# First layer's modulation on TensorE, four products at a time on quarters of its columns; all first shift tiles computed there too

## The chip, the cores and the metric

The kernel runs on one core of a Trainium2 chip. The metric is device time in microseconds, from the start of the program to its end. A core has five engines that work side by side, each through its own queue in order: PE (TensorE, matrix products), DVE (VectorE), ACT (ScalarE), POOL (GpSimd) and SP (SyncE, which here issues the loads). Loads run on 16 DMA engines. Smaller is better.

## The reference

Two transformer blocks of two layers each work on 256 latent tokens and 256 context tokens of width 1024, batch 1. Each layer derives six modulation vectors (shift, scale and gain for the mixer; the same for the feed-forward) from a conditioning vector, once for the latents (c) and once for the context (c_ctx). The first block's mixer is a bidirectional mLSTM beside a gated spatial unit and a convolution; the second block's are attention layers. The part that the change touches is the first layer's first lines:

```
c_act = jax.nn.silu(c)
cc_act = jax.nn.silu(c_ctx)
mod = (c_act @ w_mod[l] + b_mod[l])[:, None, :]
modc = cc_act @ w_mod[l] + b_mod[l]
sh1, sc1, g1, sh2, sc2, g2 = jnp.split(mod, 6, axis=-1)
shc1, scc1, gc1, shc2, scc2, gc2 = jnp.split(modc, 6, axis=-1)
px = (rmsnorm(x, norm1_g[l]) * (1.0 + sc1) + sh1) @ w_in[l] + b_in[l]
pc = (rmsnorm(xc, norm1_g[l]) * (1.0 + scc1) + shc1) @ w_in[l] + b_in[l]
```

All is float32. The projections are computed with both operands split into a high and a low half, three products each.

## The kernel before

The activations lie transposed, channels on partitions: xT is eight tiles [128, 512], the first 256 columns the context tokens, the rest the latents. A modulation vector of 1024 entries is eight tiles of 128 entries (j = 0 to 7 in each of the six parts c of a layer), one entry per partition. There are two ways of computing a tile. `mod_tile` (line 155) loads 128 rows of the transposed weights (512 KB) and takes two dot products on VectorE (line 165, one for each stream) with the conditioning vector spread over all partitions (`cv`). `mod_pe` (line 171) does two tiles for both streams on TensorE: it loads two blocks of 512 KB (line 177), adds up eight products over the channels in float32 (line 180; each product shows as two records), in which the stationary operand has only two columns, the two conditioning vectors; ScalarE copies the resulting two rows (line 182), two transpositions turn them onto the partitions (line 184), and `mod_take` adds the bias and makes the norm's gain (lines 191 and 196).

`start` (line 198) is everything ahead of the first mixer. It loads xT, squares it and sums (lines 212 and 217), spreads the two conditioning vectors over the partitions with products of ones (`cvec_pe`, line 138), and computes scale and shift of the first norm in four steps q of two tiles. All four steps' scales and the shifts of q = 1 (`SHPE`) go over TensorE, five calls of mod_pe; the other six shift tiles are dot products on VectorE. The 512 KB blocks of both kinds share eight buffers. The factors of the norm come from the sums of squares (line 323), a chain of small VectorE operations (from line 294) and a product that spreads them (line 331); xT times the factors is xr (line 242). Then for each of the eight tiles k of channels ScalarE applies scale and shift (line 255), and the result is split into aH (line 378) and aL (line 379). Three weight tiles of the input projection are loaded in the midst of it and split (whi, line 392; wlo, line 397).

The mixer (`mixer1`, line 590) begins with three tiles of the input projection, gates, k0 and k1, whose products (lines 411 to 413, 512 tokens each, named pin) are taken k by k as aH and aL come, 72 in all. The gates then go through a chain of running sums and maxima on VectorE (lines 727 to 755), whose result is transposed on TensorE (line 764). Its constants are loaded from line 597 on into memory that `start` has used, so they wait for its last aL. The rest of the mixer follows the list PLAN. One of its items, `mods`, put behind other work by a priority lowered by 300, calls mod_pe four times for part 4, the scale of the feed-forward's norm; its buffers are the two of `mw`.

The framework orders each engine's instructions ahead of time, by priority (program order, unless changed) and by a cost model's estimate of when operands are ready. Within an engine the order is then fixed. Modulation tiles of later use are queued (`mod_queue`, `work`) and put behind the last split or residual on VectorE (the fence).

## Time and profile before

| | us |
|---|---|
| median of 3 runs | 2062.37 |
| lowest, highest | 2057.48, 2063.44 |
| span of the profiled execution | 2055.1 |

The profiled execution's span runs from its first to its last instruction. The profile gives, for each engine, what it did when, what ended its idle time, and the chain of work that ended last. "x16" counts instructions; a float32 product shows as two records. In rows of the timeline the first number is the start and the second the time to the end of the last one, so neighbouring pipelined products overlap in their durations, and the distance of two starts is what one of them takes of the engine's time. In the rows of stretches each engine has its busy time and its count. The clock column is the granted clock of TensorE as a share of full speed, the last two columns are the load of the DMA engines.

### The profile page before, as it was taken

What the parts mean: (1) busy time and instruction counts of PE and PEld (TensorE: products, weight loads), DVE (VectorE), ACT (ScalarE), POOL (GpSimd) and SP (SyncE); (2) the same over time, 40 slices, a digit from 0 to 9 for tenths busy, and PEclk for the clock granted to TensorE, in tenths of its full rate; (3) what the DMA queues carried; (4) which work ended last, traced back from release to release, by engine and by line L of the source; (5) the groups of instructions that cost most, each with busy time, mean ns of one, the idle gap of its engine ahead of it and who ended that gap; (6) DMA issues with size and microseconds to landing.
All of it is one profiled execution on the core that took longest, in us unless ns stands there. A gap on an engine that the chain in (4) does not pass through costs nothing.

```text
span 2055.1 us, 34137 instructions
## 1 busy us (share of the span) xinstructions
PE 2010.6 (98%) x13196; PEld 1784.5 (87%) x13196; DVE 1545.2 (75%) x3105; ACT 924.5 (45%) x1612; POOL 85.7 (4%) x103
## 2 busy tenths in 40 slices
PE   8999999999999899999999999999999999999999
PEld 3798779888888799999998789888888889999999
DVE  6997789987898768987877667777653487788554
ACT  4324544222322346744556675322222266666443
POOL 0000010000001000200100002000000200001000
PEclk9999999999999999999999999999999999999999
DMA  7532265678766332576651015446752231216554
GB/s 295 181 103 92 97 232 176 211 248 295 235 216 198 111 102 94 170 263 212 202 171 61 22 41 186 154 149 223 260 170 71 70 112 64 73 54 224 182 157 134
DMA packets 98182, 324.22 MB, mean 158 GB/s; under 512 B 11418, under 2 KB 14234, under 8 KB 98020
## 3 DMA queue, kind: packets, MB, share of 16 engines
q1 hardware_dynamic: 98020, 322.04, 47.7%
q8 instruction: 104, 1.70, 0.3%
q14 instruction: 58, 0.48, 0.1%
HBM read 320.95 MB, written 1.05 MB: 157 GB/s over the span
## 4 chain that ended last, share of the span: by engine, by line
PE 89%; DVE 6%; ACT 2%; DMA 1%; issue 1%; SPq 0%; POOL 0%; ACTq 0%; POOLq 0%; DVEq 0%
PE pg L411 6%; PE pd L411 6%; PE pd L413 6%; PE pd L412 6%; PE pu L413 6%; PE pg L412 6%; PE pu L412 6%; PE pg L413 6%; PE pu L411 6%; PE pin L411 5%; PE pin L413 5%; PE pin L412 5%; PE pov L1223 2%; PE ptq L1127 2%; DVE wlo L397 1%; PE po L411 1%
## 5 line engine op out<-in xcount | busy, mean ns | idle before, releaser
L392 ACT CAST whi<-wraw 128x1024 fp32r<-128x1024 f32 (+2 forms) x443 | 429.5, 973 | 797.0 <-PE pu L412 188.9
L397 DVE TENSOR_TENSOR wlo<-wraw,whi 128x1024 fp32r<-128x1024 f32 (+2 forms) x443 | 502.5, 1138 | 155.0 <-ACT whi L392 152.3
L165 DVE CUSTOM_DVE_ANT_0 junk<-mw,cv,modb 128x1024 bf16<-128x1024 f32 x272 | 349.6, 1285 | 51.3 <-DMA mw<-in_modw 45.2
L411 PE MATMUL pd<-hH,whi 128*128 128x256 f32 (+1 forms) x748 | 245.4, 328 | 0.0
L412 PE MATMUL pd<-hL,whi 128*128 128x256 f32 (+1 forms) x748 | 245.1, 328 | 0.0
L413 PE MATMUL pd<-hH,wlo 128*128 128x256 f32 (+1 forms) x748 | 244.8, 327 | 0.0
L411 PE MATMUL pg<-aH,whi 128*128 128x256 f32 (+1 forms) x704 | 233.8, 332 | 0.3 <-ACT aH L374 0.3
L413 PE MATMUL pu<-aH,wlo 128*128 128x256 f32 (+1 forms) x704 | 233.5, 332 | 0.3 <-DVE wlo L397 0.3
L412 PE MATMUL pg<-aL,whi 128*128 128x256 f32 (+1 forms) x704 | 233.6, 332 | 0.0
L412 PE MATMUL pu<-aL,whi 128*128 128x256 f32 (+1 forms) x704 | 233.2, 331 | 0.0
L411 PE MATMUL pu<-aH,whi 128*128 128x256 f32 (+1 forms) x704 | 233.2, 331 | 0.0
L413 PE MATMUL pg<-aH,wlo 128*128 128x256 f32 (+1 forms) x704 | 233.2, 331 | 0.0
L412 PEld LDWEIGHTS pd<-hL,whi 128*128 128x128 f32 x748 | 142.2, 190 | 12.2
L411 PEld LDWEIGHTS pd<-hH,whi 128*128 128x128 f32 x748 | 142.4, 190 | 12.0
L413 PEld LDWEIGHTS pd<-hH,wlo 128*128 128x128 f32 x748 | 142.2, 190 | 12.0
L411 PE MATMUL pin<-whi,aH 128*128 128x256 f32 x512 | 150.0, 293 | 1.4 <-ACT aH L374 1.1
L412 PE MATMUL pin<-wlo,aH 128*128 128x256 f32 x512 | 148.0, 289 | 0.0
L413 PE MATMUL pin<-whi,aL 128*128 128x256 f32 x512 | 147.2, 289 | 0.3 <-DVE aL L375 0.2
L411 PEld LDWEIGHTS pg<-aH,whi 128*128 128x128 f32 x704 | 133.7, 190 | 13.2 <-ACT aH L374 0.5
L413 PEld LDWEIGHTS pu<-aH,wlo 128*128 128x128 f32 x704 | 133.7, 190 | 13.1 <-DVE wlo L397 0.5
L413 PEld LDWEIGHTS pg<-aH,wlo 128*128 128x128 f32 x704 | 133.8, 190 | 12.6
L412 PEld LDWEIGHTS pg<-aL,whi 128*128 128x128 f32 x704 | 133.8, 190 | 12.5
(339 smaller groups left out, 4150.8 us busy)
## 6 DMA issues: line engine op xcount, KB each, us to landing
wraw<-in_wgu SPq DMA_DIRECT2D x176, 512.0 KB, 4.4
mw<-in_modw SPq DMA_DIRECT2D x168, 512.0 KB, 4.2
wraw<-in_win SPq DMA_DIRECT2D x92, 512.0 KB, 3.5
wraw<-in_wdn SPq DMA_DIRECT2D x64, 384.0 KB, 3.5
wraw<-in_wout SPq DMA_DIRECT2D x47, 512.0 KB, 3.5
wraw<-in_wdn SPq DMA_DIRECT2D x64, 320.0 KB, 3.4
mn<-in_modn SPq DMA_DIRECT2D x18, 512.0 KB, 5.6
mn<-in_modw SPq DMA_DIRECT2D x6, 512.0 KB, 7.3
```

Of the source, the lines that this page charges most:

```text
L165: r = nc.vector.tensor_tensor_reduce(out=junk, in0=w, in1=self.cv[s], scale=1.0, scalar=self.mb_t[:, 2 * b + l, j:j + 1], op0=ALU.mult, op ...
L392: nc.scalar.copy(out=hi[:, :n], in_=raw[:, :n])
L397: nc.vector.tensor_tensor(out=lo[:, :n], in0=raw[:, :n], in1=hi[:, :n], op=ALU.subtract)
L411: mm(out=out, lhsT=wh, rhs=xh, start=start, stop=False)
L412: mm(out=out, lhsT=wh, rhs=xl, start=False, stop=False)
L413: mm(out=out, lhsT=wl, rhs=xh, start=False, stop=stop)
L1127: nc.tensor.transpose(out=pt[:, h, :], in_=a.bitcast(F32).rearrange("p e d -> p (e d)"), identity=self.ident)
L1223: nc.tensor.matmul(out=po[64 * b:64 * b + 64, e // 2, :], lhsT=vN[:, kc, 64 * g:64 * g + 64], rhs=u["PT"][:, kc, :], start=kc == 0, stop=k ...
```

## The change

The products of mod_pe go to quarters of TensorE's columns. The stationary operand becomes 32 columns wide, the two conditioning vectors and 30 columns of zeros (`columns`, built once in start and once in mods), and the four products of a block write to four groups of 32 partitions, each of which adds up over the two blocks only. The copy takes all 128 partitions, and instead of a transposition a product with a constant of two columns (`quart`) adds the four quarters and turns the rows. All eight shift tiles of the first norm are computed in this way, so that start makes eight calls of mod_pe and no dot product; their order is no longer tied to the product that spreads the factors. The sums alternate between two banks instead of halves of one. The spreading of the conditioning vectors on TensorE goes; the two spread vectors, which later tiles need, are loaded as broadcasts at the end of start. Three constants are loaded through ScalarE's queue instead of SP's, ahead of the Silu of the small conditioning columns. Comments are dropped as well.

```diff
-CS = {"ident": (0, 128), "mf": (128, 128), "mb": (256, 128)}
-NCS = 384
+CS = {"ident": (0, 128), "mf": (128, 128), "mb": (256, 128), "quart": (384, 2)}
+NCS = 386
...
-SHPE = (1,)
...
-        self.cols = g.tile([128, 4 * KT], F32, name="cols")
+        self.cols = g.tile([128, KT, 2], F32, name="cols")
         nc.sync.dma_start(out=self.cols, in_=i["ccol"])
-        nc.scalar.activation(out=self.cols, in_=self.cols, func=AF.Silu)
         self.cst = g.tile([128, NCS], F32, name="cst")
-        nc.sync.dma_start(out=self.cst, in_=i["cst"])
+        nc.scalar.dma_start(out=self.cst, in_=i["cst"])
         self.ident = self.C("ident")
         self.gn = g.tile([128, 9, KT], F32, name="gn")
-        nc.sync.dma_start(out=self.gn, in_=i["gn"])
+        nc.scalar.dma_start(out=self.gn, in_=i["gn"])
         self.mb_t = g.tile([128, 4, 48], F32, name="modb")
-        nc.sync.dma_start(out=self.mb_t, in_=i["modb"])
+        nc.scalar.dma_start(out=self.mb_t, in_=i["modb"])
+        nc.scalar.activation(out=self.cols, in_=self.cols, func=AF.Silu)
...
-    def cvec_pe(self, s, row):
...
+    def columns(self, pool):
+        t = pool.tile([128, KT, 32], F32, name="cols32")
+        self.nc.gpsimd.memset(t, 0.0)
+        self.nc.vector.tensor_copy(out=t[:, :, 0:2], in_=self.cols)
+        return t
...
-    def mod_pe(self, c, q, room, pr, pm):
+    def mod_pe(self, cols, c, q, room, pr, pm):
         nc = self.nc
         for h in range(2):
             w = room()
             nc.sync.dma_start(out=w, in_=self.i["modn"][PE_C.index(c), q, h])
             for n in range(4):
-                k = 4 * h + n
-                nc.tensor.matmul(out=pr, lhsT=self.cols[:, 2 * k:2 * k + 2], rhs=w[:, 256 * n:256 * n + 256], start=k == 0, stop=k == KT - 1)
-        row = self.np_.tile([128, 256], F32, tag="xn", name="mrow")[0:2, :]
+                nc.tensor.matmul(out=pr[32 * n:32 * n + 32, :], lhsT=cols[:, 4 * h + n, :], rhs=w[:, 256 * n:256 * n + 256],
+                                 start=h == 0, stop=h == 1)
+        row = self.np_.tile([128, 256], F32, tag="xn", name="mrow")
         nc.scalar.copy(out=row, in_=pr)
         for j in (0, 1):
-            nc.tensor.transpose(out=pm[:, 2 * (2 * q + j):2 * (2 * q + j) + 2], in_=row[:, 128 * j:128 * j + 128], identity=self.ident[0:2, 0:2])
+            nc.tensor.matmul(out=pm[:, 2 * (2 * q + j):2 * (2 * q + j) + 2], lhsT=row[:, 128 * j:128 * j + 128], rhs=self.C("quart"),
+                             start=True, stop=True)
...
-            rows = [mf.tile([1, D], F32, name=f"crow{s}") for s in range(2)]
-            for s, row in enumerate(rows):
-                nc.sync.dma_start(out=row, in_=self.i["cvec"][s:s + 1, :])
+            pR = [pR, self.ps.tile([128, T], F32, tag="aux", bufs=1, name="pR1")]
...
-            for s, row in enumerate(rows):
-                self.cvec_pe(s, row)
...
-            def scale(q):
-                for c in (1, 0) if q in SHPE else (1,):
-                    half[0] = 1 - half[0]
-                    self.mod_pe(c, q, room, pR[0:2, 256 * half[0]:256 * half[0] + 256], pM[:, 16 * c:16 * c + 16])
-                    self.mod_take(c, 2 * q, 2 * q + 2, pM[:, 16 * c:16 * c + 16])
-            def shift(j):
-                if j // 2 not in SHPE:
-                    self.mod_tile(0, 0, j, (1, 0), room())
-            for j in range(2):
-                shift(j)
-            scale(0)
+            cols = self.columns(mf)
+            def part(c, q):
+                half[0] = 1 - half[0]
+                self.mod_pe(cols, c, q, room, pR[half[0]][:, 0:256], pM[:, 16 * c:16 * c + 16])
+                self.mod_take(c, 2 * q, 2 * q + 2, pM[:, 16 * c:16 * c + 16])
+            part(1, 0)
+            part(0, 0)
             npb = self.rstd_rows([acc], T, 1.0 / D, pc, pb)
...
             for q in range(4):
-                with self.tc.issue_after(npb.ins):
-                    if q:
-                        scale(q)
-                for j in (2 * q, 2 * q + 1):
-                    if j >= 2:
-                        shift(j)
+                if q:
+                    part(1, q)
+                    part(0, q)
...
+        self.cvecs(0)
...
             def mods():
                 pm = self.mm_tile("pm")
+                cols32 = self.columns(tp)
                 for q in range(4):
-                    self.mod_pe(4, q, lambda: self.mp.tile([128, D], F32, tag="mw", bufs=2, name="mn"), pm[0:2, 0:256], pm[:, 256:272])
+                    self.mod_pe(cols32, 4, q, lambda: self.mp.tile([128, D], F32, tag="mw", bufs=2, name="mn"), pm[:, 0:256], pm[:, 256:272])
                 self.mod_take(4, 0, KT, pm[:, 256:272])
...
+    for n in range(4):
+        for st in range(2):
+            cst[32 * n + st, 384 + st] = 1.0
```

## Rows read from the trace of the kernel before

**Rows 1.** The page: busy us, share, instructions by engine; shares of the last chain.

```profile
PE 2010.6 (98%) x13196; PEld 1784.5 (87%) x13196; DVE 1545.2 (75%) x3105; ACT 924.5 (45%) x1612; POOL 85.7 (4%) x103
...
PE 89%; DVE 6%; ACT 2%; DMA 1%; issue 1%; SPq 0%; POOL 0%; ACTq 0%; POOLq 0%; DVEq 0%
```

**Rows 2.** Busy time by stretch (stretch, its length, engines, granted clock, DMA share, GB/s).

```profile
core 0: us, PE busy (x) PEld busy (x) DVE busy (x) ACT busy (x) POOL busy (x), PEclk, DMA share, GB/s
...
16.00:20.00 4.00, 3.74 (x11) 1.52 (x12) 3.90 (x7) 0.00 (x0) 0.00 (x0) 1.00 1.02 410
...
32.60:57.90 25.30, 25.30 (x111) 16.27 (x110) 20.92 (x37) 12.40 (x23) 1.31 (x10) 1.00 0.53 194
...
57.90:80.00 22.10, 17.44 (x73) 12.87 (x72) 21.22 (x36) 9.65 (x13) 0.00 (x0) 1.00 0.56 188
...
80.00:266.00 186.00, 186.00 (x1151) 152.36 (x1152) 157.63 (x389) 78.40 (x136) 2.52 (x2) 1.00 0.34 110
```

**Rows 3.** Timeline, TensorE in the start (start us, us, engine, line, operation, names, count).

```profile
14.77 1.86 PE L323 MATMUL npc<-ones,sqa 128*128 128x1 f32 x8 [3.25 <-DVE sqa L217]
...
16.89 5.87 PE L180 MATMUL pR<-mn,cols 128*2 128x256 f32 x16 [0.26 <-DMA mn<-in_modn]
...
23.22 0.28 PE L184 MATMUL pM<-cst,mrow 2*128 2x2 f32 x2 [0.45 <-ACT mrow L182]
...
24.48 3.62 PE L180 MATMUL pR<-mn,cols 128*2 128x256 f32 x16
...
32.63 0.50 PE L411 MATMUL pin<-aH,whi 128*128 128x512 f32 x1
...
57.41 0.39 PE L412 MATMUL pin<-aL,whi 128*128 128x512 f32 x1
...
57.63 0.39 PE L413 MATMUL pin<-aH,wlo 128*128 128x512 f32 x1
```

**Rows 4.** Timeline, issues of loads on SP's queue in the start.

```profile
3.26 3.67 SPq L210 DMA_DIRECT2D xT<-in_xT  x8
...
14.29 2.90 SPq L391 DMA_DIRECT2D wraw<-in_win  x3
```

**Rows 5.** Timeline, VectorE in the start.

```profile
14.63 1.28 DVE L165 CUSTOM_DVE_ANT_0 junk<-mn,cv,modb 128x1024 bf16<-128x1024 f32 x1
...
19.82 0.16 DVE L294 TENSOR_SCALAR nw_a<-npc 128x4 f32<-128x4 f32 x1
...
29.38 1.28 DVE L379 TENSOR_TENSOR aL<-xn,aH 128x512 fp32r<-128x512 f32 x2
...
30.66 1.21 DVE L397 TENSOR_TENSOR wlo<-wraw,whi 128x1024 fp32r<-128x1024 f32 x1
```

**Rows 6.** Timeline, TensorE: one column, half columns, and the two full-width groups after them.

```profile
211.15 1.62 PE L323 MATMUL pcv<-ones,csq 128*128 128x1 f32 x14
...
218.24 1.09 PE L924 MATMUL psg<-sws,vs 128*64 128x128 f32 x16
...
219.26 1.09 PE L862 MATMUL pht<-cst,hs 128*128 128x128 f32 x8
...
221.24 1.16 PE L839 MATMUL U<-va,ks 128*128 128x129 f32 x8
```

**Rows 7.** TensorE: busy time of line 180 by stretch; timeline of part 4's records.

```profile
205.00:270.00 65.00, 17.37 (x64) 3.60 (x64) 1.00 0.33 109
...
222.33 2.75 PE L180 MATMUL pm<-mn,cols 128*2 128x256 f32 x12
...
254.49 0.59 PE L180 MATMUL pm<-mn,cols 128*2 128x256 f32 x2
...
255.02 0.38 PE L411 MATMUL po<-aH,whi 128*128 128x256 f32 x1
```

**Rows 8.** Timeline, TensorE: its longest wait between 58 and 80 us.

```profile
77.68 0.28 PE L764 MATMUL ptr<-cst,RT 100*128 100x100 f32 x1 [3.31 <-issue]
```

**Rows 9.** Waits on SP's queue up to 60 us (us in total, times, longest).

```profile
SPq L597 <- DVE aL L379: 15.1, 1, 15.1
```

More of the change, by code (lines that the diff above doesn't have):

```diff
@@ L130, in cvec @@
         nc.scalar.activation(out=t, in_=t, func=AF.Silu)
-    def cvec_pe(self, s, row):
-        nc = self.nc
-        t = self.cv[s] = self.mp.tile([128, D], F32, tag="cv", name=f"cv0{s}")
-        for h in range(2):
-            p = self.mm_tile("pcv")
-            nc.tensor.matmul(out=p, lhsT=self.ones[0:1, :], rhs=row[0:1, 512 * h:512 * h + 512], start=True, stop=True)
-            nc.scalar.activation(out=t[:, 512 * h:512 * h + 512], in_=p, func=AF.Silu)
     def cvecs(self, b):
@@ L1517, in lay @@
     cc = np.stack([f("c")[0], f("c_ctx")], axis=1)
-    out["ccol"] = np.concatenate([cc.reshape(KT, 128, 2).transpose(1, 0, 2).reshape(128, 2 * KT)] * 2, axis=1)
+    out["ccol"] = cc.reshape(KT, 128, 2).transpose(1, 0, 2)
     mb = np.stack([f("b_mod"), f("mod_b_2")]).reshape(4, 48, 128)
```

## The prediction

> **What bounds the kernel now.** I read the shares of the page first: the matrix engine (TensorE, PE) is busy 98% of the span and is 89% of the chain that ended last [rows 1]. So PE time that goes away is time gained wherever PE has no gap, and nothing elsewhere. The view of busy time by stretch says where that is [rows 2]. From 32.6 to 57.9 us, and from 80 to 266, PE is busy the whole stretch. Between 57.9 and 80 it stands still for 4.7 us, and the timeline names the longest piece: 3.31 us ahead of a transposition (L764) that waits for the gates' running sums on VectorE [rows 8]. Both places that the change touches lie in stretches without a gap: the end of the start (to 57.9), and the modulation's part 4 (205 to 270).
>
> Now the start in order of time. A "part" is one call of mod_pe: two tiles of one modulation vector, 1 MB of weights, 16 records on PE. The first takes 5.87 us, the others (five in all) 3.62 [rows 3]. The granted clock column reads 1.00 in that stretch too [rows 2], but 0.226 us a record is the pace of 2.4 GHz, and the first part's mean of 0.37 means that most of its records ran at the lower of the two levels, 1.2 GHz. PE had done little but 1.86 us of sums shortly before. The first product of the input projection starts at 32.63; the last one of the first three tiles at 57.63, so it ends at 57.86 [rows 3]. These 25.2 us hold 72 products at 0.227 (two neighbouring starts give 0.22), 16.3 us, two parts with their turning, 2 x (3.62 + 0.21) = 7.7, and 1.2 of restarts after each part. Nothing starves PE there, so the gates' evacuation follows PE.
>
> What sets 32.63? The low half of the first weights is made at 30.66 to 31.87, after the two aL of 29.38, and PE is then in a part until 32.7 [rows 3, 5]. The aL wait for the norm's factors, whose first operation starts at 19.82 although its sums were done at 14.77 + 1.86 = 16.63: four dot products of the shifts, from 14.63 on, stood ahead of it on VectorE [rows 3, 5]. The weights are the ninth to eleventh 512 KB loads on SP's queue, and the transfer runs at its ceiling, some 410 GB/s, meanwhile [rows 2, 4].
>
> **The part's new price.** No row shows four quarters side by side. The nearest are halves: 16 records of 64 columns take 1.02 us from start to next start (218.24 to 219.26), 64 ns each, while 8 of the same length on all columns take 1.09, 136 ns each [rows 6]. Two halves therefore overlap fully. For quarters the bounds are 3.62 (none overlap) and 3.62/4 = 0.91; pairs only would be 1.81. I take 1.1, near the low end, since the halves lost nothing. The turning changes from two records (0.28 with its tail, 0.21 to the next start) to two products with 128 rows and columns, two records each: at 1.62/14 = 0.116 that is 0.46, at the slow level 4 x 1.86/8 = 0.93 [rows 3, 6]. A part comes to **1.55 us** against 3.83 (bounds 1.3 and 4.1).
>
> The Trainium skill (TensorE: Matmul & The Clock Gate, Measured speedup vs the span model) gives 3.07 times for four row tiles and 2.38 for three column tiles; an estimate from that page, 3.62/3.07 = 1.2 us, would move the sum below by 0.7.
>
> **Start (A).** Removed: six shift tiles on VectorE, twelve dot products of 1.28 us, and the spreading of the two vectors over PE. Added: three parts on PE (eight instead of five). Loads for them: the same 512 KB each, so no bytes change. The norm's first operation no longer stands behind dot products, 19.82 to about 16.7, and xT's loads are issued about 2 us sooner, because three constants move to ScalarE's queue and two rows go [rows 4, 5]. That also brings the three weights 2 us sooner. I put the first product at 29.0; it cannot be much ahead of 27 (the weights' landing and two conversions), nor has it a reason to be later than 32.6. The loads of the last eight tiles stand behind the three weights on SP's queue, as the later ones do now, so four parts remain after the first product: 29.0 + 16.3 + 4 x 1.55 + 1.5 restarts = 53.0, **4.9 us** sooner than 57.86. Best: 27 + 16.3 + 5.2 + 1.0 = 49.5, 8.4 gained. Worst with overlap: 32.6 + 16.3 + 4 x 2.3 + 1.5 = 59.6, 1.7 lost.
> Nothing: the zeroed columns and their copy (two short instructions on GpSimd and VectorE, which wait for xT then), the constants' issues on ScalarE (0.46 each, as xT's eight show [rows 4], ahead of its first square, which waits for xT anyway), three more short row copies, and the two broadcast loads at the end (2.6 us of transfer at 410 GB/s, with their Silu) as long as they lie behind the last tile; in front of it they push it by 2.6.
> The mixer's constants wait on SP for the start's last aL, 15.1 us now [rows 9]. No dot product stands ahead of that aL any more, so I let it come 7 us sooner, and they land before the gates need them.
>
> **Behind the start (B).** Dot products of the queue are fenced behind the last aL. If it comes 7 us sooner and the gates only 5, so one or two more of them (1.28 each) are done before the gates' chain, on which PE waits 3.31 [rows 8]. I take **1.0**, bounds 0 and 3.
>
> **Part 4 in the mixer (C).** 64 records, 17.37 us busy [rows 7]. The timeline shows two patterns: 28 stand in runs (12, 6, 6, 4; the run of 12 takes 2.75), 36 in pairs of 0.59, each between single products po [rows 7]. A pair is one matmul. If the order stays alternating, a lone quarter takes its full length and a quarter of the array does its work: no gain. Runs: 28 x 0.226 = 6.3 falls to 1.9, 4.4 gained; turning costs 4 x (0.46 - 0.28) = 0.7. I take **3.7**. Bounds: -0.7 (none stand together) and 14.5 - 4.4 + about 3 for interruptions - 0.7 = 12.4 (all together).
> The Trainium skill (TensorEngine Tiling (Array Packing), Key Properties) says a change of tiling mode drains the engine, which speaks against quarters strewn among full-width products. In the row of 255.02 the next product starts 0.53 after a pair that needs 0.45, a cost that is already paid for unpacked pairs; by the rule C would be at its lower bound.
>
> **Sum.** A 4.9 + B 1.0 + C 3.7 = 9.6. The profiled execution has a span of 2055.1, 7.3 under the median of the runs; what lies around the span stays. 2062.4 - 9.6 = **2052.8**. About 0.3%, 6.2 us, is what a measurement of this kernel can tell from no change.
>
> **Rivals.**
> - All four quarters of part 4 run together: C = 12.4, 2044.1. For it: in the start all 16 stand together. Against: the alternation [rows 7].
> - The start ends on loads, part 4 gives nothing: rooms for the last tiles come free late, SP puts the vectors and other weights ahead of them, the last part is 5 us later and A is 2.9 at most; C = -0.7; total 3.2, 2059.2. For it: PE would be less full than now, and transfers run at the ceiling [rows 2].
> - The clock: parts of 1.5 us paced by 1 MB loads (2.6 us at 410 GB/s) leave PE waiting between them, where it now works through. The first part shows the price, 2.3 us for one stay at the low level [rows 3]; two such stays take 4.6: 2057.4. Against: the 72 products are dense. The Trainium skill (TensorE: Matmul & The Clock Gate, Part 1) has the low level as the idle default, which speaks for this rival; the row of the first part agrees.
> - Slower: quarters run one after another, the change doesn't do what it says. A part is 3.62 + 0.46 = 4.1 and the start ends at 29 + 16.3 + 16.3 + 1.5 = 63.1, 5.2 later; C costs 0.7: 2068.3. It decides once a part costs more than (57.86 - 29 - 16.3 - 1.5)/4 = 2.8. Against: the halves [rows 6].
>
> **Chances.** Forecast 0.45, all together 0.14, loads 0.20, clock 0.13, one after another 0.08. Faster by over 0.3% (under 2056.2): nearly all of the first two and a little of the clock's, 0.61. Within 0.3%: 0.29. Slower: the last and some accident of order, 0.10. The 8-in-10 range leaves out the last case and the tails: 2044 to 2064.
>
> **What would show it.** Right: 16 records of a part within 1.3 us; first pin product near 29; last of the first three tiles near 53; the wait of L764 no longer than 3.3; part 4's 64 records under 13 us. Wrong: parts near 3.6; equal records spaced double after 25 us; PE idle between parts after 32; the same pairs between po with the chain no shorter from 200 to 266.

## The result, and the profile of the changed kernel

The changed kernel takes 2072.2 us (2069.3 to 2074.6), the kernel before 2059.8 (2057.5 to 2063.4) in the same session: a ratio of 1.0053, interval 1.0039 to 1.0066. By the medians it is slower by 12.4 us. The forecast was 2052.8, faster by 9.6; sign and range were both wrong.

The page first, the lines that answer to [rows 1].

```profile
PE 2010.9 (97%) x13266; PEld 1795.9 (87%) x13266; DVE 1529.7 (74%) x3086; ACT 923.4 (45%) x1612; POOL 82.0 (4%) x105
...
PE 86%; DVE 9%; ACT 2%; issue 2%; DMA 1%; POOL 0%; SPq 0%; POOLq 0%; DVEq 0%; ACTq 0%
```

TensorE is busy as long as before (2010.6), although records went away, and VectorE's share of the chain rose from 6% to 9%. Busy time alone hides two things here: how long PE waits, and how much of its busy time ran at the lower clock. So I split each stretch in three, from the view of busy time in pieces of 10 us: idle is length less PE's busy time; clock is the sum of busy time x (1 - granted clock); work is the rest, what the records would take at full clock. Beside the changed kernel stands a second profiled execution of the kernel before (e9 below); the first one has idle 44.5, clock 10.0, work 2000.5.

```
us                    kernel before, again         changed kernel
                      length  idle clock   work    length  idle clock   work
start to first ptr      78.6  13.8   0.3   64.5      83.3  26.6   1.1   55.5
to first pinB           19.3   0.0   4.6   14.7      23.4   0.0   5.1   18.3
to first pg            216.2   4.0   1.4  210.8     214.0   8.3   5.5  200.2
to first pov           788.9  13.0   4.2  771.7     797.8  13.2  11.1  773.5
to the end             956.8  13.9   4.4  938.5     954.1  13.6   1.4  939.1
sum                   2059.8  44.7  14.9 2000.2    2072.6  61.7  24.2 1986.6
```

This table is the case. The change does what it says: 13.6 us of TensorE work are gone, more than the 9.6 I had hoped for. But 17.0 us of waiting and 9.3 of low clock came in their place. The waits grew where the work went away: 12.8 in the start, 4.3 in the mixer. By length, the changed kernel loses 8.8 us up to the first pinB, wins 2.2 in the mixer, and loses 8.9 behind the first pg, where no instruction was changed; 6.9 of that is clock.

Two things in the start's row are to be read with care. Of its 12.8 us, 5.7 stand before 10 us: there TensorE was busy 5.74 us with spreading the vectors, and now it waits for the first sums, which start at 13.45, no later than before (14.77, [rows 3]); so these 5.7 cost nothing. And the clock column misses a part: it reads 1.00 from 30 to 40 us, though the twelve products from 33.46 to 39.28 take 5.8 us, and twelve take 2.7 at the pace of 0.23 that the later ones have. Some 3 us of the start's work therefore belong under clock (e2 below has the same start, and its profile reads 0.66 there).

The same stretches as [rows 2], in the changed kernel:

```profile
core 0: us, PE busy (x) PEld busy (x) DVE busy (x) ACT busy (x) POOL busy (x), PEclk, DMA share, GB/s
16.00:20.00 4.00, 3.11 (x16) 1.13 (x8) 1.78 (x10) 0.37 (x1) 0.00 (x0) 1.00 1.02 416
32.60:57.90 25.30, 23.78 (x134) 14.23 (x134) 7.08 (x13) 12.80 (x23) 0.00 (x0) 1.00 0.42 156
57.90:80.00 22.10, 16.98 (x65) 13.09 (x65) 17.45 (x25) 12.44 (x16) 1.31 (x10) 0.92 0.55 180
80.00:266.00 186.00, 180.77 (x1139) 154.94 (x1139) 160.25 (x385) 74.61 (x131) 2.20 (x3) 0.97 0.36 113
```

TensorE had no gap in the second and the last of them; now it has 1.5 and 5.2 us of gaps, and the granted clock is under 1 in two. Of the 5.2, 3.3 are the wait for ptr, which stood before 80 us in the kernel before and now reaches past it.

TensorE's timeline in the start, to be laid beside [rows 3]:

```profile
15.22 1.93 PE L177 MATMUL pR<-mn,cols 128*32 128x256 f32 x16
...
23.11 1.01 PE L182 MATMUL pM<-cst,mrow 128*128 128x2 f32 x4 [0.49 <-ACT mrow L180]
...
33.46 0.79 PE L399 MATMUL pin<-aH,whi 128*128 128x512 f32 x1 [1.82 <-ACT whi L380]
...
39.28 0.91 PE L177 MATMUL pR<-mn,cols 128*32 128x256 f32 x8
...
51.95 0.64 PE L177 MATMUL pR<-mn,cols 128*32 128x256 f32 x8
...
53.88 0.64 PE L177 MATMUL pR<-mn,cols 128*32 128x256 f32 x8
...
62.21 0.39 PE L401 MATMUL pin<-aH,wlo 128*128 128x512 f32 x1
...
66.44 0.47 PE L399 MATMUL pin<-aH,whi 128*128 128x512 f32 x1 [3.84 <-DVE FG L649]
```

Sixteen records of a part take 1.93 us, against 5.87 and 3.62. The last four parts, though, stand as eight halves about 2 us apart among the first tiles' products, from 39.28 to 53.88; the kernel before had its last pR at 44.8. The first product is at 33.46, not earlier than before (32.63). ScalarE shows why:

```profile
30.20 0.37 ACT L180 COPY mrow<-pR 128x256 f32<-128x256 f32 x1 [2.46 <-PE pR L177]
31.87 0.60 ACT L242 ACTIVATE xn<-xr,mod,modA 128x256 f32<-128x256 f32 x1 [1.30 <-DVE mod L190]
32.38 1.03 ACT L380 CAST whi<-wraw 128x1024 fp32r<-128x1024 f32 x1
```

The same two steps in the kernel before stand the other way round:

```profile
28.73 2.93 ACT L392 CAST whi<-wraw 128x1024 fp32r<-128x1024 f32 x3
...
34.50 1.58 ACT L255 ACTIVATE xn<-xr,mod,modA 128x256 f32<-128x256 f32 x3 [1.41 <-DVE mod L191]
```

In the changed kernel the first weights' conversion (32.38) is queued behind the normalisation of tile k = 2, which waits for the second round's shift. That shift came over TensorE before, too; what is new is that it stands ahead of the conversion. In e2, with the same start and the same wait, the first product is at 31.42, so some 2 of the 33.46 seem to belong to this one execution. And VectorE at the start's end, with the last aL:

```profile
60.09 0.69 DVE L367 TENSOR_TENSOR aL<-xn,aH 128x512 fp32r<-128x512 f32 x1 [1.27 <-ACT aH L366]
...
62.57 2.36 DVE L385 TENSOR_TENSOR wlo<-wraw,whi 128x1024 fp32r<-128x1024 f32 x2 [1.79 <-ACT whi L380]
...
64.85 0.73 DVE L648 TENSOR_SCALAR G<-pin,pv 36x512 f32<-36x512 f32 x1
```

The last aL and the gates' evacuation in the kernel before:

```profile
52.04 0.69 DVE L379 TENSOR_TENSOR aL<-xn,aH 128x512 fp32r<-128x512 f32 x1 [0.71 <-ACT aH L378]
...
56.70 0.74 DVE L660 TENSOR_SCALAR G<-pin,pv 36x512 f32<-36x512 f32 x1
```

Both come some 8 us later now, and two conversions stand in front of the gates' evacuation. PE waits for it 3.84 us, and then 4.32 in front of the first ptr (3.31 before, [rows 8]). Two more waits stand in the mixer:

```profile
83.28 0.28 PE L752 MATMUL ptr<-cst,RT 100*128 100x100 f32 x1 [4.32 <-DVE RT L736]
...
237.53 0.91 PE L801 MATMUL st<-qT,kT 128*128 128x128 f32 x6 [1.35 <-DVE so L851]
...
287.44 0.59 PE L311 MATMUL npc<-ones,sqa 128*128 128x1 f32 x2 [3.67 <-POOL sqa L335]
```

### The profile page after: what moved, and what is told of

The parts are those of the page before. It is cut to its first block, busy times and chain, and to the rows that moved or that the text cites. A ratio compares the mean times of both kernels' runs of the same rounds, so it can differ in the third digit from the quotient of the medians.

```text
span 2072.6 us, 34262 instructions
## 1 busy us (share of the span) xinstructions
PE 2010.9 (97%) x13266; PEld 1795.9 (87%) x13266; DVE 1529.7 (74%) x3086; ACT 923.4 (45%) x1612; POOL 82.0 (4%) x105
## 4 chain that ended last, share of the span: by engine, by line
PE 86%; DVE 9%; ACT 2%; issue 2%; DMA 1%; POOL 0%; SPq 0%; POOLq 0%; DVEq 0%; ACTq 0%
PE pg L399 6%; PE pu L401 6%; PE pg L401 6%; PE pu L399 6%; PE pu L400 6%; PE pg L400 6%; PE pd L399 6%; PE pd L400 6%; PE pd L401 6%; PE pin L399 5%; PE pin L401 4%; PE pin L400 4%; DVE wlo L385 2%; PE pov L1212 2%; PE ptq L1116 2%
## 5 line engine op out<-in xcount | busy, mean ns | idle before, releaser
L400 PEld LDWEIGHTS pd<-hL,whi 128*128 128x128 f32 x748 | 141.6, 189 | 12.3
L400 PEld LDWEIGHTS pu<-aL,whi 128*128 128x128 f32 x704 | 133.7, 190 | 12.5
```

The lines of the kernel that those rows point to most:

```text
L400: mm(out=out, lhsT=wh, rhs=xl, start=False, stop=False)
```

## The experiments

All times are medians; the kernel before lies between 2058.9 and 2060.9 in the sessions.

**Which half loses?** e1 packs part 4 alone, in the kernel before; e2 packs the start alone.

```diff
 e1: def mods():
-    self.mod_pe(4, q, ...)
+    self.mod_pe4(cols32, 4, q, ...)      # the new function; start() keeps the old one
 e2: the changed kernel, with in mods()
-    self.mod_pe(cols32, 4, q, ...)
+    self.mod_pe1(4, q, ...)              # the old function
```

> The kernel before with one part of the change: only the four calls for part 4 in the mixer run on quarters; the start is that of before. Theory 'order' (the loss arises in the start, where the planner strews the halves of the last four calls between the products of the first three tiles, so that the last aL comes 8 us later, 60.8 instead of 52.7): part 4 alone gains 3 to 4 us, ratio to before 0.998. Rival 'part 4' (strewn quarters drain the engine and cost the time in the mixer): slower by 5 us or more, ratio 1.003 or above. Rival 'clock' (thinner work on TensorE lets its clock fall): about 0.998 to 1.001, no new low-clock stretch in the first 110 us.

> The changed kernel with part 4 in the mixer as before (eight products of two columns and transpositions); the start is the changed one. Theory 'order': the whole loss and the missing gain of part 4 together, ratio to before 1.006 to 1.008, first pinB product some 13 us later than in before. Rival 'part 4': about as fast as before, 0.998 to 1.001. Rival 'clock': as 'order', with low granted clock from 60 to 100 us.

e1: 2063.6, ratio 1.0021 (1.0009 to 1.0032). e2: 2068.3, 1.0049 (1.0029 to 1.0068). Both halves lose, the start more. In e2 the last pR is at 51.7 and the last aL at 57.6, with PE waits of 3.85 and 4.33 as in the changed kernel. In e1 the start is unchanged, and from the first pinB to the first pg it has work 203.0 (7.8 less), idle 7.7 (3.7 more) and clock 6.5 (5.1 more): 217.2 us where the kernel before took 216.2. So C's gain was there and was paid back on the spot. The rest of e1's loss stands behind the first pg: 795.9 us to the first pov, against 788.9.

**Is it the moved shift tiles, or the packing?** e3 packs in both places and leaves the six shift tiles on VectorE. e4 is the changed kernel with the first three tiles' products queued behind the last part on TensorE.

```diff
 e4: first three tiles of mixer1
-    self.accA(p3, w3, (self.aH, self.aL), cs)
+    with self.tc.issue_after(self.last_pe):   # the last part's turning
+        self.accA(p3, w3, (self.aH, self.aL), cs)
```

> Quarters in both places, but the work is divided as before: five calls in the start, six shift tiles as dot products on VectorE, conditioning vectors spread by TensorE, constants on SP's queue. Theory 'order': five calls of about 1.5 us in place of 3.8 leave the last aL no later than 52.7, faster than before by 4 to 8 us, ratio 0.996 to 0.998. Rival 'clock': with less work on TensorE ahead of them the first products run at the low level and the loss stays, ratio 1.003 or above.

> The changed kernel with one constraint more: the products of the first three tiles are queued on TensorE behind the last of the start's eight calls, so that no half of a call stands between them. Theory 'order': the last call ends near 42, the last aL comes near 47 instead of 60.8, the three tiles end near 59, the gates' evacuation follows at once (the wait of 3.8 us behind it is under 1), ratio to before 0.998 to 1.001 in place of 1.005. Rival 'clock': TensorE waits more ahead of 40 us, so the products begin at the low level, and the ratio stays at 1.004 or above.

e3: 2065.2, 1.0033 (1.0020 to 1.0046). Its start holds 8.7 us less TensorE work than the kernel before (55.8 against 64.5), and its first ptr stands at 78.2 (78.6): nothing came of it; idle is 19.3 (13.8) and clock 3.2 (0.3). e4: 2073.9, 1.0077 (1.0063 to 1.0090). Its last pR is at 46.0 and its last aL at 52.4, as in the kernel before, but now all 72 products follow, and the view by stretch shows at which level:

```profile
30.00:40.00 10.00, 4.73 (x38) 2.25 (x31) 5.22 (x7) 6.47 (x11) 0.00 (x0) 0.50 1.02 407
40.00:50.00 10.00, 8.23 (x48) 5.13 (x49) 1.95 (x6) 5.42 (x12) 0.00 (x0) 0.50 0.04 17
50.00:60.00 10.00, 10.00 (x40) 8.11 (x39) 1.39 (x2) 3.33 (x5) 1.32 (x10) 0.85 0.46 158
```

With little to do from 30 to 40 TensorE runs at the lower level and stays there while it catches up. Its longest wait there, 4.78 us up to 36.18, ends on ScalarE's copy of a part's rows, and ScalarE is busy 5.97 of the 6 us from 30 to 36. From the last parts' order alone nothing was to be had in this form. At this point I took the clock for nearly the whole cause, because the first profile of the kernel before had so little of it.

**Is the clock the cause?** Useless products go into TensorE's longest waits, in the changed kernel (e6), in e3 (e7) and in the kernel before (e8). They are ordered in front of the waiting instruction and need nothing late themselves. e9 profiles the kernel before once more.

```diff
 e6, in front of the first transposition to ptr (and likewise behind the first tiles and in front of npc)
+    for _ in range((13, 5)[l] if c == 0 else 0):
+        nc.tensor.matmul(out=p, lhsT=self.aH[0][:, 0:128], rhs=self.aH[0], start=True, stop=True)
```

> The changed kernel with products that nobody reads put into four of TensorE's waits: 16 behind the first three tiles (wait of 3.84 us at 66.44), 13 in front of the first ptr of mixer 1 (4.32 at 83.28), 6 in front of npc (3.67 at 287.44), 5 in front of ptr in the second mixer (3.90 at 729.84). They add some 10 us of work to TensorE and remove nothing. Theory clock (the waits let the granted clock fall, and the low level afterwards costs the time): the low stretches behind these waits, worth 1.4 + 0.3 + 2.9 + 2.3 us at 60 to 100, 2.2 + 3.3 + 1.4 at 280 to 310 and 4.8 at 730, go for the most part; the median falls from 2072.2 to 2053 to 2063. Theory order (the start's chain ends some 5 us later and the rest follows it): the added work lies in waits, so nothing moves: 2070 to 2075. Rival that the fill is simply work: 2076 to 2083.

> Products packed in both places, shift tiles left on VectorE (2065.2 as measured), with the same useless products in the waits: 8 behind the first three tiles, 12 in front of ptr, 6 in front of npc, 5 in front of the second mixer's ptr. Clock theory: the low stretches at 50 to 90 (4.3 us), 280 to 300 (5.1) and 730 (5.2 with 720) mostly go: 2049 to 2058, at or below the kernel before. Rival (the clock falls whatever these waits hold): 2064 to 2069.

> The kernel before, with 12 useless products in front of ptr (its wait is 3.31), 4 in front of npc (1.67) and 5 in front of the second mixer's ptr (3.93). Clock theory: what it loses behind these waits is 1.7 us at 280 and 5.1 at 710 to 730 in the profiled execution, so 2053 to 2057 against 2058.9. Rival: 2058 to 2063, no gain or the work added.

> The kernel before, unchanged, profiled once more, to see whether the granted clock falls at the same places. If the falls belong to the order of the instructions alone, they stand at 280, 710 to 730, 1640 to 1660 and 1840 again, and none follows the wait of 3.31 us in front of ptr at 77.68. If they are drawn anew in each execution, the places differ: one may follow that wait, worth some 3 us there, and the span moves by the same.

e6: 2072.6, the same as without. e7: 2071.5, 6.3 worse than e3. e8: 2064.0, 1.0017 (1.0006 to 1.0028); its trace is not read here. The theory fell as a cure. In e6 the fall at 60 to 80 is gone and the clock term before the first pg goes from 11.7 us to 5.4, but the products did not stay in the waits:

```profile
84.16 0.28 PE L765 MATMUL ptr<-cst,RT 100*128 100x100 f32 x1 [1.68 <-DVE RT L746]
87.20 2.61 PE L757 MATMUL pmi<-mi,sel 4*128 4x4 f32 x16 [2.51 <-DVE mi L753]
...
287.30 0.58 PE L311 MATMUL npc<-ones,sqa 128*128 128x1 f32 x2 [4.33 <-POOL sqa L337]
294.57 2.83 PE L344 MATMUL npb<-sq 128*128 128x256 f32 x12 [1.15 <-DVE so L864]
```

The wait moved on to pmi, and those meant for npc ended behind it, where they cost their full length. e9 then corrected the baseline. It ran 2061.6, and the same wait that had no fall behind it in the first profile has one here:

```profile
78.57 0.40 PE L764 MATMUL ptr<-cst,RT 100*128 100x100 f32 x1 [3.28 <-issue]
...
70.00:80.00 10.00, 6.72 (x28) 5.31 (x27) 9.67 (x18) 1.78 (x3) 0.00 (x0) 0.88 0.31 107
80.00:90.00 10.00, 10.00 (x40) 7.97 (x40) 5.49 (x17) 4.33 (x5) 0.00 (x0) 0.61 0.31 105
```

Two executions of one kernel differ by 4.7 us of span, and 4.6 of it stands right here. The profile on which the prediction rests was a lucky one; the falls at 80 in e1 and e3 were none of their doing. What remains of the clock is the 9.3 in the table above. It is not the accident of one execution: the granted clock is 0.986 to 0.988 in all five runs of the changed kernel, and 0.990 to 0.995 in 89 runs of the kernel before. The middle values, 0.987 and 0.993, of some 2011 busy us make an estimated 12 us. So the new waits cancel the work that was saved, and the lower clock is most of what the kernel lost. So the question became where the 17 us of waiting come from.

**What does the start wait for?** DMA's share is 1.01 to 1.03 from 10 to 40 us in both kernels. e10 and e11 leave out half of the loads for the modulation in the start.

```diff
 e11 (e10 likewise, shift tiles in pairs too)
-    w = room()
-    nc.sync.dma_start(out=w, in_=self.i["modn"][PE_C.index(c), q, h])
+    if h == 0 or c == 4:
+        w = room()
+        nc.sync.dma_start(out=w, in_=self.i["modn"][PE_C.index(c), q, h])
```

> The kernel before with 8 of the 16 tiles of 512 KB that the start loads for its modulation left out (one tile is read twice in its place, so the first layer's scales and shifts are other numbers; every product and dot product is still there). 4.2 MB less at the 390 to 410 GB/s of the stretch 10:40 is some 10 us of loading less. Theory loads (in the start of the kernel before, DMA and TensorE are both full, so that neither alone can bring much): 1 to 4 us are gained, 2056 to 2059. Theory TensorE (the prediction's own: its products are the path there): nothing, 2059 to 2061.

> The changed kernel with the same 8 loads left out (one tile read twice for both halves of a call in the start). Theory loads: with TensorE's part of the start packed, the loads (share of the DMA engines 1.01 to 1.03 from 10 to 40) are what its 26.6 us of idle time in front of the first ptr wait for; without half of them the last aL comes 8 to 10 us earlier than 60.8, and the median falls by 7 to 11, to 2061 to 2065: a larger gain than the same loads bring in the kernel before. Theory order (the last four calls stand strewn among the first tiles' products whenever their loads land): 0 to 3 us, 2069 to 2073.

e10: 2057.8, 0.9989 (0.9978 to 1.0001), 1.8 us under the kernel before, not clear of no change. e11: 2060.3, 1.0005 (0.9993 to 1.0017), 11.9 us under the changed kernel. In e11 the last pR is at 37.6 instead of 53.9, and the rest follows (VectorE, then TensorE):

```profile
45.10 0.69 DVE L368 TENSOR_TENSOR aL<-xn,aH 128x512 fp32r<-128x512 f32 x1 [1.27 <-ACT aH L367]
...
71.91 0.28 PE L753 MATMUL ptr<-cst,RT 100*128 100x100 f32 x1 [3.06 <-DVE RT L737]
```

The first ptr moves from 83.28 to 71.91; in e10 it stays (80.3 against 78.6). So with packed parts the start hangs on its loads, or on the order that is made for them, while with unpacked ones taking TensorE's work or the loads away alone (e3, e10) is worth little. The order on TensorE is laid out anew when loads go, so e11 doesn't part their time from the order; e17 below changes the order alone. The changed kernel's own trace says that both count: DMA's share is 1.01 from 40 to 42 us and 0.04 from 44 to 46, while the last halves stand until 53.88 and TensorE has no gap. From 44 on it is the order that holds them:

```profile
40.00:50.00 10.00, 10.00 (x72) 5.82 (x72) 0.49 (x3) 2.81 (x7) 0.00 (x0) 1.00 0.31 123
```

And the start's gain doesn't reach the end. From e10 to e11, with half the loads in both, the change brings the first ptr 8.4 us forward, yet e11's median lies 2.5 above e10's; 5.2 us are lost again behind the first pg (795.1 against 789.9).

**What does the mixer wait for?** e12 and e13 leave out eight of the background tiles, sixteen dot products on VectorE, in the kernel before and in e1. From 266 to 296 the kernel before has ten dot products in a burst; e12 has one there, e13 five.

```diff
 def mod_tile(self, b, l, j, streams, w=None):
+    if (b, l) == (0, 0) and j // 8 == 3:
+        nc.gpsimd.memset(m[:, 0:2, j:j + 1], 0.0)
+        return
```

> The kernel before without the eight tiles 24 to 31 of the first layer's modulation (16 dot products of 1.36 us on VectorE and 8 loads; the second norm's shift is zero), most of which stand between 272 and 292. Theory VectorE (a burst of dot products at the end of mixer 1 is what TensorE waits for there: 1.67, 1.54 and 0.74 us from 280 to 300): 2 to 5 us are gained, 2055 to 2058. Theory nothing: 2058 to 2061.

> The kernel with part 4 alone packed, without the same eight tiles. Theory VectorE: part 4's products had covered this burst, so that packing them bought waits (TensorE idle between the first pinB and the first pg 7.7 us against 4.0); without the burst the packing pays: 2053 to 2056, 2 to 5 us under the kernel before without the burst. Rival (clock or order): it stays 2 to 6 us above that kernel, as it is 4.7 us above the kernel before with the burst.

e12: 2053.4, 0.9969 (0.9957 to 0.9980). e13: 2044.7, 0.9931 (0.9918 to 0.9944). Without that burst part 4's packing gains 8.7 us, with it it loses 4.7. In the stretch that holds part 4, first pinB to first pg, the gain is 6.9 (203.1 against 210.0 us); the rest stands outside it, much of it clock. Busy time in the mixer's last third, two lines each, of the kernel before (e9), e1, e12 and e13 (columns as in [rows 2]):

```profile
205.00:270.00 65.00, 65.00 (x398) 45.56 (x397) 48.14 (x148) 33.21 (x70) 2.51 (x2) 1.00 0.27 93
270.00:300.00 30.00, 26.77 (x199) 25.12 (x199) 27.52 (x45) 12.93 (x19) 5.17 (x5) 0.94 0.73 251
```

```profile
205.00:270.00 65.00, 63.65 (x416) 48.59 (x414) 46.03 (x136) 31.79 (x64) 2.84 (x3) 0.95 0.28 98
270.00:300.00 30.00, 23.69 (x156) 22.60 (x156) 27.01 (x57) 10.68 (x16) 3.29 (x3) 0.83 0.63 216
```

```profile
205.00:270.00 65.00, 64.98 (x405) 45.29 (x405) 50.60 (x150) 33.31 (x68) 3.05 (x3) 1.00 0.28 100
270.00:300.00 30.00, 29.89 (x244) 29.28 (x245) 25.25 (x47) 18.28 (x30) 6.59 (x7) 1.00 0.63 224
```

```profile
205.00:270.00 65.00, 64.53 (x477) 52.22 (x476) 51.40 (x146) 36.10 (x73) 7.15 (x6) 1.00 0.38 130
270.00:300.00 30.00, 28.97 (x238) 28.46 (x237) 28.13 (x51) 19.07 (x30) 6.60 (x7) 1.00 0.62 220
```

With the burst VectorE is busy 27 of the last 30 us and TensorE only 24 to 27, the less the fewer of part 4's records are left to do meanwhile. Without it TensorE is busy nearly throughout, at full clock. VectorE's own busy time hardly shows the difference (25 and 28 us; e13's mixer ends at 297, so the window holds later work). The waits do: between the first pinB and the first pg e1 has 7.7 us in five waits of over 0.5, the longest 3.67 for npc, which ends on a GpSimd sum; e12 and e13 have one each, under 0.6. So part 4's records had been filling gaps that came with the burst.

**Can it pay with all work kept?** e14 (kernel before) and e15 (part 4 packed) hand the background tiles out earlier; e19 and e20 do that too, and put every second wlo subtraction of the mixer on GpSimd.

```diff
 e14, e15, e19, e20
-PACE = {..., "w1": 5.5, ...}
+PACE = {..., "w1": 8.0, ...}
 PLAN[0], in front of the last steps
-        ("work",), ("work",), ("step", 3, 0, False, False, True),
+        ("step", 3, 0, False, False, True),
```

> The kernel before with its background dot products in mixer 1 handed out earlier: 8.0 units of credit at each of the first four places instead of 5.5 at six, so that the last two places, in front of the last steps, hand out none. All work is kept. Theory VectorE: the kernel before covers most of the burst with part 4's products; 0 to 4 us are gained, 2055 to 2060. Rival: VectorE is full from 100 to 160 (20.0 of 20 us), and what is handed out earlier delays the steps there: 2060 to 2065.

> Part 4 alone packed, with the dot products handed out earlier in the same way. Theory VectorE: the packing pays as soon as the burst is not at the mixer's end; 2050 to 2056, 3 to 8 us under the kernel before with the same order. Rival (the dot products cost TensorE the same wherever they stand): within 2 us of the 2063.6 of part 4 alone.

> Part 4 packed, the dot products handed out earlier, and every second wlo subtraction of mixer 1's weights from the seventh on put on GpSimd, which has 12 us of work between 80 and 340. That takes some 8 of 1.23 us, 10 us, off VectorE. Theory VectorE: part of the packing's gain comes out, 2046 to 2051, and 2 to 5 us under the same kernel without the packing. Rival (GpSimd gives the subtractions late, the tiles wait for wlo instead): 2053 to 2060.

> The kernel before with the dot products handed out earlier and the same subtractions on GpSimd. Theory VectorE: without the packing TensorE is the bound there again, so little comes of it: 2050 to 2054. Rival: late subtractions, 2053 to 2060.

e14: 2053.0, 0.9965 (0.9952 to 0.9978), which beats both kernels. e15: 2053.2, 0.9968 (0.9956 to 0.9981): no gain from the packing. The theory's 3 to 8 us between the two did not come; the rival was right that the dot products cost the packing as much elsewhere, and wrong in its 2063.6. In e15 TensorE waits for VectorE earlier instead (idle 6.7 to the first pg against 2.1 in e14, with 4.6 us less work):

```profile
206.88 0.49 PE L844 MATMUL nm<-va,E 128*128 128x129 f32 x2 [1.10 <-DVE E L839]
210.70 0.62 PE L201 MATMUL pm<-mn,cols 128*32 128x256 f32 x2 [0.87 <-DVE cols L190]
228.43 0.62 PE L201 MATMUL pm<-mn,cols 128*32 128x256 f32 x2 [0.83 <-DMA mn<-in_modn]
275.58 0.66 PE L885 MATMUL pht<-cst,hs 128*128 128x128 f32 x4 [0.92 <-DVE hs L878]
```

e19: 2082.4, e20: 2089.5, both far above the kernel before (1.0102 and 1.0136). The edit moved 17 subtractions and not the 8 that I had reckoned with: GpSimd takes 2.78 us for what VectorE does in 1.23, 47 us in all, and TensorE waits elsewhere, 6.55 us for kT at 179.76 the longest. Between the two the packing is worth 7.1 us, but that is a gain in a kernel that lost 29.

**Is the start's order to blame?** e17 holds only the products of k = 4 to 7 behind the last part; e18 adds e14's edit.

```diff
 e17, first three tiles
+    self.accA(p3, w3, (self.aH[:4], self.aL[:4]), cs, True, False)
+    with self.tc.issue_after(self.last_pe):
+        for k in range(4, KT):
...
```

> The changed kernel, with the first three tiles' products of k = 4 to 7 held behind the last call's turning on TensorE and those of k = 0 to 3 left where they fall. Theory order: the last four calls then run as their loads land (last pR near 46 and last aL near 52.5, as with all products behind), while 36 products fill the wait; the three tiles end near 58 instead of 62 and the first ptr stands near 79 instead of 83.3; the median falls from 2072.2 by 3 to 5, to 2067 to 2069. Rival (the chain over ScalarE and VectorE behind the calls sets the end, whatever TensorE's order): 2071 to 2074.

> Both: the changed kernel with the first tiles' products held as above and the dot products handed out earlier. If both theories hold, the gains add: 4 us in the start and 8 to 12 in the mixer's end, 2055 to 2060, and some executions under the kernel before. If only one holds, 2062 to 2069.

e17: 2067.3, 1.0037 (1.0024 to 1.0050), 4.9 under the changed kernel. The last pR is at 49.1 instead of 53.88, the last aL at 55.59 instead of 60.09 and the wait behind the first tiles is down from 3.84 to 2.27:

```profile
61.86 0.47 PE L399 MATMUL pin<-aH,whi 128*128 128x512 f32 x1 [2.27 <-DVE FG L649]
```

The edit changes the order alone, though 2.2 us of the difference are there at the first product already (31.26 against 33.46), which the edit doesn't hold. And it is not all: the parts did not go at once as in e4, and the first ptr is at 81.3, still behind the kernel before. e18: 2073.2, 1.0062 (1.0048 to 1.0076). The two edits do not add. From the first pinB to the first pg e18 takes 225.7 us (e17 217.1, e14 209.4), of which 11.6 idle and 10.4 clock, in seven waits of 0.9 to 2.2 us that end on VectorE or ScalarE. Its mixer begins later than e14's and VectorE has the same dot products to do in what is left; that this is the reason is argued, not shown.

## Why the prediction was wrong, step by step

- **"PE time that goes away is time gained wherever PE has no gap."** This is the step that failed, in both places. [rows 1, 2] show a full TensorE, and from them I took that nothing else was near its limit, so that less work would move all that follows up. In the start the same rows had DMA at 1.02, and in the mixer VectorE at 158 of 186 us; I read the one as a pace for loads and did not read the other. In place of the 9.6 us, 13.6 of work went and 17.0 of waiting and 9.3 of low clock came. e3 (8.7 us of work gone, the first ptr 0.4 earlier), e11 and e13 show it: the gain comes only where what feeds TensorE is relieved too, in the start the loads or the order made for them, in the mixer the dot products. e15 shows that to move these isn't enough.
- **First product at 29.0.** It came at 33.46. I had argued from VectorE and the loads, and gave no reason for anything later than 32.6. ScalarE's queue was not looked at: the conversion of the first weights stands behind a normalisation that waits for a part, and stood ahead of it before (28.73).
- **The part's price, 1.55.** Right. A part's 16 records take 1.93 us at the lower level and 2 x 0.57 between neighbouring starts at the higher, 1.14 (I took 1.1); the levels are read from the paces here, since the clock column is 1.00 for both. The turning takes 0.50 warm and 1.01 cold (0.46 and 0.93). Unpacked, a part takes 3.55 from start to next start (34.63 to 38.18 before), and 3.55/1.14 is 3.1. The estimate that the Trainium skill's figure for row tiles gave (TensorE: Matmul & The Clock Gate, Measured speedup vs the span model) was 1.2 us, and the trace agrees. By that estimate the sum would have moved by some 0.5, not 0.7. The way to the 1.1 was flawed: in the comparison of halves [rows 6] 64 ns was a distance of starts and 136 a duration. From start to start the full-width eight take 116 ns each (219.26 to 220.19), so that the halves overlapped 1.8 times, not wholly.
- **Four parts and 72 products one after the other, ending at 53.0 (A, 4.9 gained).** The length was too short and the order wrong. From the first product to the end of the three tiles it took 29.0 us, not 24.0: about 3 more in the first twelve products, at the slower pace, 0.9 in a wait for aH at 58, the rest in restarts. And eight halves were strewn to 53.88, so that the last products could start only at 60. The three tiles end near 62.4, 4.6 later than before. e17 takes 4.9 us of the time back by order alone.
- **B, 1.0 gained.** It went the other way: a new wait of 3.84 behind the first tiles and 4.32 for 3.31 in front of ptr, because the gates' evacuation stands behind two wlo and the chain starts 8 us later.
- **C, 3.7 gained.** The records did shrink, from 17.37 us [rows 7] to 11.64, and lone pairs took 0.62 (0.59), with no gain, as argued. That is 5.7 us, where I had 4.4 ahead of the longer turning. It bought waits (e1) until VectorE had less to do (e13). The step that failed is not the size but that a stretch without a gap would pass it on.
- **The rivals.** "The start ends on loads" had a resource that counts, but I let it cost gain only, and its sum doesn't say why a last part 5 us later takes only 2.0 off A. Between the changed kernel and its half-loaded version lie 11.9 us (e11), with the order changed as well. "The clock" was placed in the start, at 4.6; the accounts show 9.3 more than in e9, of it 4.1 in the mixer and 6.9 between the first pg and the first pov. The slower side was given one mechanism that was not there and 0.02 for "some accident of order", which is a part of what happened (4.9 us, e17).

**What stays open.** Behind the first pg, where no instruction was changed, the clock term is 4.2 in both profiles of the kernel before and in e13 4.6, but 11.1 in the changed kernel and 7.3 to 12.3 in e1, e2, e3 and e15. It isn't the packing's own: e12 and e20, with nothing packed, have 7.6 and 8.2; and e15's runs have a granted clock of 0.990 to 0.996, as the kernel before, so that its 12.3 is that of one execution, its slowest. Three waits there are the same in the kernel before, e3, e13 and the changed kernel (1.9, 2.3 and 3.9 us between 658 and 730). A fourth is not; here it is in e9 and in the changed kernel:

```profile
853.80 0.38 PE L323 MATMUL npc<-ones,sqa 128*128 128x1 f32 x2 [1.31 <-POOL sqa L347]
...
866.53 0.59 PE L311 MATMUL npc<-ones,sqa 128*128 128x1 f32 x2 [2.58 <-POOL sqa L335]
```

In the 20 us behind it the clock term is 0.0 in e9 and 4.8 in the changed kernel, most of the 6.9. Of the other profiles, the seven in which this wait is 0.9 to 1.3 us have no fall behind it, and of the ten with 1.6 to 3.1 all but one (e12, 1.8) have one, worth 1.5 to 5.0. Why the wait for GpSimd's sum is longer in some kernels, and why waits alike have different prices, I have no experiment that says.

## What to carry to other kernels

A full engine is not a bound by itself: its work may be filling gaps that another engine or the loads make, and then cutting it buys waits, and behind waits a lower clock. Before costing such a cut, look in the same stretch for what is second (a DMA share at 1.0, VectorE at 90%), and ask what would be late if the engine had nothing to do; one run with a part of that second work left out helps to answer it, if one checks that the order of the rest stays. And where instructions lie in an order fixed ahead, shorter work does not move the others up: read the queues of every engine that feeds the first instruction, not only the one that is busiest.

## What the runs showed of the hardware

Four quarters of 32 columns run together: 16 records of 128x256 take 1.14 us at the faster of the two paces seen, where 16 unpacked ones take 3.55, and 1.93 at the slower, where 16 unpacked ones took 5.87 as the first part [rows 3]. A pair of quarters alone between full-width products takes 0.62 and gains nothing. One and the same wait of 3.3 us (77.68 and 78.57) was followed by a granted clock of 1.00 in one execution of the kernel before and by 0.88 and 0.61 in the next, 4.6 us apart: a single profile doesn't tell what a wait costs. And GpSimd needs 2.78 us for the subtraction of a 128x1024 tile that takes VectorE 1.23.
